# TensorE's order written out by hand around LayerNorm's transposes, in w_o's second pass and each layer's first FFN group

## The chip, the cores and the metric

The program runs on one core of one Trainium2 chip. Its time is the device time of one execution in microseconds (us), as the median of several runs. The engines are named as the profile names them: PE is TensorE (matmul and transpose), PEld its weight loads, DVE VectorE, ACT ScalarE, POOL GpSimd and SP the engine that issues most loads.

## What is computed

Two layers of a backbone over 1024 latent tokens of width 1024 (the first mixes by differential attention over 1024 + 256 tokens, the second by a centred pooling mixer), each followed by a SwiGLU FFN of width 2816. The parts that the change touches are the attention's output projection, LayerNorm behind it, and the FFN:

```python
def layer_norm(x, g, b):
    mu = jnp.mean(xf, axis=-1, keepdims=True)
    var = jnp.mean(jnp.square(xf - mu), axis=-1, keepdims=True)
    return ((xf - mu) * lax.rsqrt(var + LN_EPS) * g + b).astype(x.dtype)

x = layer_norm(ALPHA * x + g1 * y_lat, ln_g[i, 0], ln_b[i, 0])
x = layer_norm(ALPHA * x + g2 * swiglu(modulate(x, sh2, sc2), ffn_w_in[i], ffn_w_out[i]),
               ln_g[i, 1], ln_b[i, 1])
```

Everything is float32.

## The kernel before, in words

**Data.** The residual stream is `zT`, transposed: eight tiles of 128 features (index k or d), 1024 tokens along. Tokens are worked in two chunks of 512. A product takes float32 operands as two float32r parts, a rounded one and the rest (`parts`, L385: ACT casts the high part on L386, DVE subtracts for the low part on L387), and is three matmuls for each 128x128 block of weights (`mm3`, L669: high by high L670, high by low L671, low by high L672). `form` makes both parts of a weight half into one of three buffers `aop`; the raw weights come by SP's loads into six buffers `raw`.

**w_o.** The attention's projection runs in two passes of eight tiles d, the first over tokens 0 to 511, the second over 512 to 1023. One tile is 24 matmuls on two weight halves q; DVE adds it to `zT` (`accumulate`, L714).

**LayerNorm.** `ln_rows` takes one block of 128 tokens: eight PE transposes of `zT` into two banks `ln` (L558), statistics on DVE (L559, L562), a power on POOL (L564), `nb` on DVE (L566), and ACT writes the normalised rows `xn` (L568). `features` turns four such blocks back for one feature tile k (four transposes, L587, one bank), and ACT reads this bank twice: modulated for the FFN (L596) and as the new `zT` (L591). There are four `ln` banks, which rows and features share, and four `mm` banks for products.

**The FFN.** `ffn` runs eleven groups g of two column tiles. Each half s of a group is a two-by-two scheme of seven products p0 to p6 instead of eight, on seven forms of the modulated input, `H[0]` to `H[6]`. A product with one form is 12 matmuls. p0 and p1 need only H[0] and H[1], which come from tokens 0 to 511 (`forms_first`, L600); H[4], H[5], H[6] and later H[2] and H[3] (`forms_last`) need the rows of tokens 512 to 1023 (`forms_second`, L611). In group 0 the program therefore has p0 and p1 of both halves and then p0 and p1 of group 1's halves (`early`), and behind these `forms_second`; p4, p5, p6, p2 and p3 follow, then the output products on `quad` tiles. `Made` loads the first weights during w_o's second pass (layer 0) or the pooling mixer (layer 1) and casts their halves into `made`; in layer 0 for groups 0 and 1, in layer 1 for group 0 alone, so that there the early products take `aop` buffers.

**What sets the order.** Each engine runs its instructions in the order in which the built program holds them. A scheduler makes this order when the program is closed: it takes what its own model has as ready, by priority of the program text. An instruction of which `keep_in_program_order` is asked stands behind the instruction that the program text put before it on the same engine; this sets an order and adds no wait.

In layer 0 the text has rows 0 to 3 (`rows_of(0, 4)`) ahead of w_o's second pass, and behind each tile d of it `forms_first` for k = d and one step of `Made`.

## Time and profile before

| | |
|---|---|
| time, median of 3 runs | 2355.43 us (2353.51 to 2359.13) |
| the profiled execution's own time | 2353.65 us |
| its span | 2351.8 us |
| mean granted clock of PE | 0.984 |
| PE busy | 2253.2 us (96%), 11552 matmuls and transposes |
| DVE, ACT, POOL busy | 70%, 39%, 24% |
| the chain that ended last | PE 28%, DVE 3%, ACT 1% |

The span is the stretch of the execution that the profile covers. A row of the timeline has the start in us from the span's beginning, the duration, the engine, the line and the operation with output and input; a bracket gives the time for which the engine stood idle before it, and the instruction that ended this. A matmul's row lasts until its result is out, so that rows that follow each other overlap; the distance between two starts is what one costs. A windows row gives the busy time of each engine in one stretch; PEclk is the clock granted to PE as a share of 2.4 GHz.

### The profile page before, as it was taken

The numbers are of one execution on the slowest core, as the hardware profiler recorded it, in microseconds if no ns is written. First come the engines' busy times: TensorE is split into PE (matmuls) and PEld (weight loads), VectorE is DVE, ScalarE is ACT, GpSimd is POOL, SyncE is SP. The second block draws the span as 40 slices with busy tenths as digits, with TensorE's granted clock in tenths as the row PEclk, the third lists the DMA queues.
The fourth block names the chain that finished last, engine by engine and source line by source line (L and its number), as shares of the span: only waits on it lengthen the run. The fifth ranks groups of instructions, "written<-read, shape, count | busy, mean of one in ns | idle before, by whom it ended". The sixth has DMA issues, their size and how long they took to land. (4 is left out here: it accounts for less than half of the span.)

```text
span 2351.8 us, 30315 instructions
## 1 busy us (share of the span) xinstructions
PE 2253.2 (96%) x11552; PEld 1908.6 (81%) x11552; DVE 1641.9 (70%) x2478; ACT 927.6 (39%) x1599; POOL 567.4 (24%) x570
## 2 busy tenths in 40 slices
PE   5989999999999997999999999999799999999997
PEld 5878887999998785888887888897588888888886
DVE  6653626998996538877777777765776666666678
ACT  3213115787885346222222222436622222222242
POOL 3531312444443212111102111113031111111112
PEclk9999999999999998999999999999899999999999
DMA  7866746423221421322323222211021111111112
GB/s 287 271 197 218 237 134 185 111 82 88 77 63 69 156 72 44 99 82 90 90 90 117 90 90 89 70 35 53 18 72 54 54 54 54 52 49 52 50 50 90
DMA packets 98817, 231.50 MB, mean 98 GB/s; under 512 B 9200, under 2 KB 25712, under 8 KB 97648
## 3 DMA queue, kind: packets, MB, share of 16 engines
q1 hardware_dynamic: 76592, 205.45, 27.6%
q10 hardware_dynamic: 22080, 24.12, 3.7%
q8 instruction: 91, 1.49, 0.3%
q14 instruction: 54, 0.44, 0.1%
HBM read 201.22 MB, written 28.31 MB: 98 GB/s over the span
## 5 line engine op out<-in xcount | busy, mean ns | idle before, releaser
L386 ACT CAST aop<-raw 128x512 fp32r<-128x512 f32 x364 | 225.9, 622 | 682.2 <-PE mm L672 611.5
L670 PE MATMUL mm<-H,aop 128*128 128x512 f32 x1184 | 463.2, 391 | 11.5 <-ACT H L386 10.7
L672 PE MATMUL mm<-H,aop 128*128 128x512 f32 x1184 | 462.1, 391 | 1.2 <-DVE aop L387 1.2
L671 PE MATMUL mm<-H,aop 128*128 128x512 f32 x1184 | 462.4, 391 | 0.0
L387 DVE TENSOR_TENSOR aop<-raw,aop 128x512 fp32r<-128x512 f32 x364 | 272.2, 750 | 118.1 <-ACT aop L386 116.8
L714 DVE SCALAR_TENSOR_TENSOR zT<-mm,g,zT 128x512 f32<-128x512 f32 (+1 forms) x384 | 271.4, 722 | 69.8 <-PE mm L672 67.2
L670 PEld LDWEIGHTS mm<-H,aop 128*128 128x128 f32 x1184 | 223.3, 189 | 59.9 <-ACT H L386 12.2
L672 PEld LDWEIGHTS mm<-H,aop 128*128 128x128 f32 x1184 | 223.1, 188 | 49.7 <-DVE aop L387 3.5
L671 PEld LDWEIGHTS mm<-H,aop 128*128 128x128 f32 x1184 | 223.3, 189 | 47.2 <-DVE H L387 0.9
L670 PE MATMUL mm<-quad,aop 128*128 128x512 f32 x608 | 237.9, 391 | 1.2 <-DVE zT L714 1.1
L671 PE MATMUL mm<-quad,aop 128*128 128x512 f32 x608 | 237.1, 390 | 1.9 <-DVE quad L387 1.9
L672 PE MATMUL mm<-quad,aop 128*128 128x512 f32 x608 | 235.9, 390 | 0.0
L427 DVE TENSOR_REDUCE mx<-s 128x1 f32<-128x1280 f32 x128 | 190.5, 1490 | 49.9 <-PE s L424 44.9
L424 PE MATMUL s<-kk,qd 128*128 128x512 f32 (+1 forms) x768 | 183.2, 374 | 3.5 <-ACT e L430 2.9
L430 ACT ACTIVATE e<-s,mx 128x1280 f32<-128x1280 f32 x128 | 170.1, 1329 | 22.6 <-DVE mx L427 22.5
L793 POOL TENSOR_TENSOR s<-raw 128x512 f32<-128x512 f32 x40 | 52.8, 1319 | 486.5 <-DMA raw<-in_w_in 428.8
L424 PEld LDWEIGHTS s<-kk,qd 128*128 128x128 f32 x768 | 136.3, 191 | 28.0 <-ACT e L430 4.0
L455 PE MATMUL misc<-vv,at 128*128 128x128 f32 x1280 | 153.5, 275 | 0.5 <-ACT at L449 0.5
L455 PEld LDWEIGHTS misc<-vv,at 128*128 128x128 f32 x1280 | 148.0, 192 | 0.8 <-ACT at L449 0.8
L433 POOL TENSOR_SCALAR e<-e,sm 128x1280 f32<-128x1280 f32 x64 | 88.0, 1375 | 244.9 <-DVE sm L431 232.2
L671 PEld LDWEIGHTS mm<-quad,aop 128*128 128x128 f32 x608 | 114.2, 188 | 26.5 <-DVE quad L387 3.5
L670 PEld LDWEIGHTS mm<-quad,aop 128*128 128x128 f32 x608 | 114.2, 188 | 26.1 <-issue 1.5
(188 smaller groups left out, 4005.7 us busy)
## 6 DMA issues: line engine op xcount, KB each, us to landing
gw<-in_w_mod SPq DMA_DIRECT2D x96, 512.0 KB, 4.5
raw<-in_w_in SPq DMA_DIRECT2D x90, 512.0 KB, 3.8
raw<-in_w_out SPq DMA_DIRECT2D x48, 512.0 KB, 3.5
qd<-q_d SPq DMA_DIRECT2D x64, 256.0 KB, 5.8
kk<-k_d SPq DMA_DIRECT2D x8, 1280.0 KB, 6.3
wr<-in_w_qk SPq DMA_DIRECT2D x18, 512.0 KB, 5.7
k_d<-ot ACTq DMA_DIRECT2D x32, 256.0 KB, 4.4
q_d<-ot ACTq DMA_DIRECT2D x32, 256.0 KB, 4.9
```

The costliest lines, as they stand in the source:

```text
L386: S.copy(hi, src)
L387: (eng or V).tensor_tensor(lo, src, hi.bitcast(F32), ALU.subtract)
L424: PE.matmul(ps[:, lo_:hi_], lhsT=self.qd[:, m, s, q0:q0 + P], rhs=self.kk[:, m, lo_:hi_], start=(s == 0), stop=(s == 1))
L427: V.tensor_reduce(mx, ps[:, 0:TA], axis=AX.X, op=ALU.max, negate=True)
L430: S.activation(e, ps[:, 0:TA], AF.Exp, bias=mx, accum_out=sm)
L433: G.tensor_scalar(e, e, sm, 1.0, ALU.mult, ALU.mult)
L455: PE.matmul(av, lhsT=self.at[:, kb, :], rhs=self.vv[:, kb, :], start=(kb == 0), stop=(kb == NTT - 1))
L670: PE.matmul(p_, lhsT=wh, rhs=xh, start=first, stop=False)
L671: PE.matmul(p_, lhsT=wh, rhs=xl, start=False, stop=False)
L672: PE.matmul(p_, lhsT=wl, rhs=xh, start=False, stop=last)
L714: V.scalar_tensor_tensor(zT[:, d, cs], p_, gate[:, d:d + 1], zT[:, d, cs], ALU.mult, ALU.add)
L793: G.tensor_tensor(S1, r1[:, 0:4], r1[:, 4:8], ALU.add)
```

## The change

Four things in the text, all on PE's order; no arithmetic is changed, added or removed.

- `pin` asks for the text's order on the transposes and on `mm3`'s matmuls while `pinned` is set.
- In w_o's second pass, rows 0 and 1 follow tile d=0, rows 2 and 3 tile d=1, and the features follow from tile d=2 on (two feature tiles each at d=2 and d=3, then one each).
- In group 0 of each layer's FFN, rows 4 and 5 stand behind the first p0, rows 6 and 7 behind both[0]'s p1, the features of i=0 and 1 behind both early p0, those of i=2 and 3 behind both[1]'s p1.
- `forms_456` is split off `forms_second` and stands ahead of the last early p1.

```diff
@@ -533,6 +533,12 @@
         return psL.tile([P, 512], F32, name="ln", tag="ln")
 
     zT = pz.tile([P, KT, T], F32, name="zT", tag="zT")
+    pinned = [False]
+
+    def pin(ins):
+
+        return tc.keep_in_program_order(ins) if pinned[0] else ins
+
     chunk = [slice(0, 512), slice(512, 1024)]
 
     def ct():
@@ -555,7 +561,7 @@
         for hf in range(2):
             p_ = lbank()
             for j in range(4):
-                PE.transpose(p_[:, j * P:(j + 1) * P], zT[:, hf * 4 + j, t0:t0 + P], ident)
+                pin(PE.transpose(p_[:, j * P:(j + 1) * P], zT[:, hf * 4 + j, t0:t0 + P], ident))
             V.bn_stats(st[:, hf, :], p_)
             pp.append(p_)
         mv = pf.tile([P, 2], F32, name="mv", tag="mv", bufs=4)
@@ -584,7 +590,7 @@
     def features(rows, k):
         p_ = lbank()
         for t, r in enumerate(rows):
-            PE.transpose(p_[:, t * P:(t + 1) * P], r[:, k * P:(k + 1) * P], ident)
+            pin(PE.transpose(p_[:, t * P:(t + 1) * P], r[:, k * P:(k + 1) * P], ident))
         return p_[:, 0:len(rows) * P]
 
     def to_x(k, cs, li, p_):
@@ -608,13 +614,12 @@
             to_x(k, chunk[0], li, p_)
             put(H, k % 4, k // 4, H[2][:, k, :], G)
 
-    def forms_second(li, M, H):
-
-
-        rows = rows_of(4, 8)
-        H[3] = phh.tile([P, KT, 512], F32, name="hB", tag="H3")
-        H[5:7] = [h_form(s) for s in range(5, 7)]
-        for i in range(4):
+    def forms_second(li, M, H, rows, idx):
+
+
+        if H[3] is None:
+            H[3] = phh.tile([P, KT, 512], F32, name="hB", tag="H3")
+        for i in idx:
             for k in (i, i + 4):
                 p_ = features(rows, k)
                 modulated(H[3][:, k, :], k, p_, M)
@@ -622,7 +627,9 @@
             t2, h12, h22 = H[2][:, i, :], H[3][:, i, :], H[3][:, i + 4, :]
             V.tensor_tensor(t2, h12, t2, ALU.subtract)
             V.tensor_tensor(t2, h22, t2, ALU.subtract)
-        H[4] = h_form(4)
+
+    def forms_456(H):
+        H[4:7] = [h_form(s) for s in range(4, 7)]
         for i in range(4):
             put(H, i, 4, H[2][:, i, :])
         for i in range(4):
@@ -667,9 +674,9 @@
         return gt
 
     def mm3(p_, wh, wl, xh, xl, first, last):
-        PE.matmul(p_, lhsT=wh, rhs=xh, start=first, stop=False)
-        PE.matmul(p_, lhsT=wh, rhs=xl, start=False, stop=False)
-        PE.matmul(p_, lhsT=wl, rhs=xh, start=False, stop=last)
+        pin(PE.matmul(p_, lhsT=wh, rhs=xh, start=first, stop=False))
+        pin(PE.matmul(p_, lhsT=wh, rhs=xl, start=False, stop=False))
+        pin(PE.matmul(p_, lhsT=wl, rhs=xh, start=False, stop=last))
 
     class Made:
 
@@ -738,12 +745,17 @@
         if d in (1, 4):
             gemv(1, d // 4)
     g2 = gate_vector(0, 5, "g2_0")
-    rows = rows_of(0, 4)
     made = Made(0, True)
+    rows = []
     for d in range(KT):
         w_o(d, 512, 512)
-        forms_first(0, M0, H, rows, [d])
+        pinned[0] = True
+        if d < 2:
+            rows += rows_of(2 * d, 2 * d + 2)
+        else:
+            forms_first(0, M0, H, rows, [range(0, 2), range(2, 4), [4], [5], [6], [7]][d - 2])
         made.step()
+    pinned[0] = False
 
     def ffn(l, gate, li, M, H, made, beside=None, after=None):
         class Half:
@@ -868,23 +880,34 @@
             if g == 0 or last:
 
                 both = [Half(2 * g, s, sg) for s in range(2)]
-                for h in both:
-                    h.p0()
-                sg0 = ct()
-                o = [h.p1_(ct() if h.s else None, sg0) for h in both][1]
                 if last:
+                    for h in both:
+                        h.p0()
+                    sg0 = ct()
+                    o = [h.p1_(ct() if h.s else None, sg0) for h in both][1]
                     keep = phh.tile([P, 2, 2, 512], F32R, name="keep", tag="H0")
                     for j in range(2):
                         S.copy(keep[:, j], at[1][j])
                 else:
 
+                    pinned[0] = True
                     early = [Half(2, s, None) for s in range(2)]
-                    for h in early:
-                        h.p0()
+                    early_forms = bool(early[0].forms)
+                    both[0].p0()
+                    rows = rows_of(4, 6)
+                    both[1].p0()
+                    sg0 = ct()
+                    both[0].p1_(None, sg0)
+                    rows += rows_of(6, 8)
+                    early[0].p0()
+                    early[1].p0()
+                    forms_second(li, M, H, rows, range(0, 2))
+                    o = both[1].p1_(ct(), sg0)
+                    forms_second(li, M, H, rows, range(2, 4))
                     early_sg = ct()
-                    early_o = [h.p1_(ct() if h.s else None, early_sg) for h in early][1]
-                    forms_second(li, M, H)
-                    early_forms = bool(made.forms.get((1, 0, 0)))
+                    early[0].p1_(None, early_sg)
+                    forms_456(H)
+                    early_o = early[1].p1_(ct(), early_sg)
                 if last:
                     for h in both:
                         h.sums()
@@ -900,6 +923,7 @@
                 for h in both:
                     h.p2()
                 at += [h.p3() for h in both][1]
+                pinned[0] = False
             else:
                 sg += [quad(F32), quad(F32)]
                 for s in range(2):
```

PE in w_o's second pass, at its beginning. L558 (L564 in the changed text) are the transposes of rows, L587 (L593) those of features; onH is the attention's output. Before:

```order
L672 MATMUL mm<-onH_2693,aop 128x512
L558 MATMUL ln<-ident,zT 128x128 x16
L670 MATMUL mm<-onH_2695,aop 128x512
...
L558 MATMUL ln<-ident,zT 128x128 x4
L670 MATMUL mm<-onH_2695,aop 128x512
L558 MATMUL ln<-ident,zT 128x128 x8
L671 MATMUL mm<-onH_2696,aop 128x512
```

In the changed program:

```order
L679 MATMUL mm<-onH_2695,aop 128x512
L564 MATMUL ln<-ident,zT 128x128 x16
L677 MATMUL mm<-onH_2695,aop 128x512
...
L564 MATMUL ln<-ident,zT 128x128 x16
L677 MATMUL mm<-onH_2695,aop 128x512
...
L593 MATMUL ln<-ident,xn 128x128 x8
```

The first 16 transposes stood directly behind the first pass and the second 16 within tile d=0; now one whole tile of 24 matmuls stands ahead of each 16, and another ahead of the first features.

PE in group 0 of layer 0's FFN. H is a form, made a weight half. Before, behind eight products:

```order
L672 MATMUL mm<-H_7570,made 128x512
L558 MATMUL ln<-ident,zT 128x128 x32
L587 MATMUL ln<-ident,xn 128x128 x32
L670 MATMUL mm<-H_8197,aop 128x512
L671 MATMUL mm<-H_8197,aop 128x512
```

In the changed program, with products between (12, then 24, then 24, then 12 matmuls, of which each "..." leaves out the rest):

```order
L677 MATMUL mm<-H_7653,made 128x512
...
L564 MATMUL ln<-ident,zT 128x128 x16
L677 MATMUL mm<-H_7653,made 128x512
...
L564 MATMUL ln<-ident,zT 128x128 x16
...
L593 MATMUL ln<-ident,xn 128x128 x16
L677 MATMUL mm<-H_7654,made 128x512
...
L593 MATMUL ln<-ident,xn 128x128 x16
```

The 64 transposes stood in one piece behind all eight products; now they are four blocks of 16 with products between them, and two products stand behind the last block.

ACT in group 0 of layer 1's FFN. L783 (L795) copies p0's result, L827 (L839) is the Silu, hB the modulated rows, the numbered H are H[4] (14248), H[5] (14249) and H[6] (14250), aop a weight half. Before:

```order
L783 COPY ct<-mm 128x512
L386 CAST aop<-raw 128x512 x2
L827 ACTIVATE ct<-ct 128x512
L386 CAST aop<-raw 128x512
L568 ACTIVATE xn<-ln,nb,mv 128x512 x8
L596 ACTIVATE hB<-ln,bm_13312,gm_13310 128x512
L591 ACTIVATE zT<-ln,lnb,lng 128x512
```

In the changed program:

```order
L602 ACTIVATE hB<-ln,bm_13312,gm_13310 128x512
L597 ACTIVATE zT<-ln,lnb,lng 128x512
L839 ACTIVATE ct<-ct 128x512
L386 CAST H_14248<-h 128x512 x4
L386 CAST H_14249<-hB 128x512 x4
L386 CAST H_14250<-h 128x512 x3
L386 CAST aop<-raw 128x512 x2
L386 CAST quad<-ct 128x512
```

The halves of p4's weights (aop), cast ahead of the eight xn before, now stand behind the hB and zT evictions and behind eleven casts of H.

## Rows read from the trace of the kernel before

**Rows 1.** The page, part 1: busy time, share and instructions.

```profile
PE 2253.2 (96%) x11552; PEld 1908.6 (81%) x11552; DVE 1641.9 (70%) x2478; ACT 927.6 (39%) x1599; POOL 567.4 (24%) x570
```

**Rows 2.** Windows, layer 0 (busy us of each engine, PEclk, DMA share, GB/s).

```profile
800.00:810.00 10.00, 5.28 (x19) 4.36 (x18) 5.17 (x13) 1.00 (x3) 4.93 (x5) 0.66 0.11 40
820.00:830.00 10.00, 10.00 (x49) 8.25 (x48) 5.17 (x7) 6.33 (x12) 2.71 (x2) 1.00 0.38 108
...
880.00:890.00 10.00, 5.71 (x34) 4.99 (x32) 6.85 (x17) 2.79 (x4) 1.11 (x2) 0.75 0.00 0
...
900.00:910.00 10.00, 4.79 (x16) 3.38 (x14) 9.63 (x17) 10.00 (x19) 0.00 (x0) 0.66 0.00 1
```

**Rows 3.** Windows, layer 1.

```profile
1670.00:1680.00 10.00, 5.87 (x23) 3.79 (x21) 8.18 (x13) 10.00 (x17) 0.00 (x0) 0.50 0.01 2
1680.00:1690.00 10.00, 8.70 (x25) 6.63 (x26) 9.13 (x16) 8.21 (x17) 0.00 (x0) 0.64 0.00 0
```

**Rows 4.** Timeline of PE, layer 0 (start, us, line, operation, idle before).

```profile
799.29 1.03 PE L558 MATMUL ln<-ident,zT 128*128 128x128 f32 x8
805.04 1.97 PE L558 MATMUL ln<-ident,zT 128*128 128x128 f32 x8 [4.72 <-DVE zT L714]
...
858.23 0.48 PE L670 MATMUL mm<-H,made 128*128 128x512 f32 x1
...
880.13 1.91 PE L558 MATMUL ln<-ident,zT 128*128 128x128 f32 x16
886.03 3.68 PE L558 MATMUL ln<-ident,zT 128*128 128x128 f32 x16 [3.99 <-ACT xn L568]
892.31 4.01 PE L587 MATMUL ln<-ident,xn 128*128 128x128 f32 x20 [2.60 <-ACT xn L568]
...
905.55 0.79 PE L670 MATMUL mm<-H,aop 128*128 128x512 f32 x1 [5.21 <-ACT H L386]
...
908.97 0.40 PE L671 MATMUL mm<-H,aop 128*128 128x512 f32 x1
...
937.34 0.39 PE L670 MATMUL mm<-quad,aop 128*128 128x512 f32 x1
...
943.65 0.50 PE L671 MATMUL mm<-quad,aop 128*128 128x512 f32 x1 [0.48 <-DVE quad L387]
```

**Rows 5.** Timeline of PE, layer 1.

```profile
1634.81 0.48 PE L670 MATMUL mm<-H,made 128*128 128x512 f32 x1
...
1681.30 0.79 PE L670 MATMUL mm<-H,aop 128*128 128x512 f32 x1 [4.75 <-ACT H L386]
...
1686.91 0.51 PE L670 MATMUL mm<-H,aop 128*128 128x512 f32 x1
...
1721.57 0.50 PE L671 MATMUL mm<-quad,aop 128*128 128x512 f32 x1 [1.46 <-DVE quad L387]
```

**Rows 6.** Timeline of DVE, layer 0.

```profile
803.63 0.69 DVE L803 TENSOR_TENSOR raw<-raw 128x512 f32<-128x512 f32 x1 [5.52 <-POOL raw L711]
804.24 0.75 DVE L714 SCALAR_TENSOR_TENSOR zT<-mm,g,zT 128x512 f32<-128x512 f32 x1
...
894.97 0.69 DVE L623 TENSOR_TENSOR h<-hB,h 128x512 f32<-128x512 f32 x1 [2.64 <-ACT hB L596]
...
905.56 2.49 DVE L387 TENSOR_TENSOR H<-h,H 128x512 fp32r<-128x512 f32 x4
```

**Rows 7.** Timeline of ACT, layer 0.

```profile
829.78 0.62 ACT L386 CAST made<-raw 128x512 fp32r<-128x512 f32 x1 [1.61 <-DMA raw<-in_w_in]
...
885.20 2.79 ACT L568 ACTIVATE xn<-ln,nb,mv 128x512 f32<-128x512 f32 x4 [6.16 <-DVE mv L563]
...
894.16 0.78 ACT L596 ACTIVATE hB<-ln,bm,gm 128x512 f32<-128x512 f32 x1
...
904.78 2.27 ACT L386 CAST H<-h 128x512 fp32r<-128x512 f32 x4
```

**Rows 8.** Timeline of SP's issues, layer 0.

```profile
825.35 0.33 SPq L693 DMA_DIRECT2D raw<-in_w_in  x1
```

## Prediction

> **What bounds the kernel now.** I read the page's busy shares first: TensorE (PE) is busy 96% of the span [rows 1], so only the places where PE waits, or runs at a low clock, can give anything. The table of 10 us windows shows where they are in layer 0: one around 800, where PE is busy 5.28 of 10 us, and one from 880 to 910, with 5.71 to 4.79, both with granted clocks of 0.66 to 0.75; at 820, in between, PE is full at clock 1.00 [rows 2]. Layer 1 has one such place; its worst windows are those from 1670 to 1690 [rows 3]. They are the places where LayerNorm turns rows on PE, and the PE timeline names each wait: 4.72 us for DVE's zT at 805, then 3.99 for xn, 2.60 for xn and 5.21 for H between 880 and 906 [rows 4]; in layer 1, 4.75 for H at 1681 [rows 5]. The rows of DVE and ACT say what stands behind these waits [rows 6, 7].
>
> **Unit prices.** A product is 12 matmuls. From the first FFN matmul at 858.23 to the first transpose at 880.13 PE runs 8 products [rows 4], so 21.90 / 96 = 0.228 us a matmul and 2.74 us a product. A block of 16 transposes takes 1.91 us and one of 8 takes 1.03 [rows 4]: 0.88 for 8 more, 0.11 each. Where the clock is down the same block of 8 takes 1.97 [rows 4]. A DVE pass over 128x512 starts every 0.60 us and an ACT cast every 0.52 (four in 2.49 and in 2.27, the last one with an overhang of 0.1 to 0.2) [rows 6, 7]. The 16 evictions of the second forms (hB and zT in turn) run from 894.16 to 904.78, 0.66 each [rows 7].
>
> **The change, stage by stage.** No instruction is added or removed. SP's and POOL's orders are the same in both programs; PE's order changes, and with it DVE's and ACT's, which the scheduler still makes. For each stage I take the time that PE needs if it never waits, the loss before, and the loss that I expect to stay.
>
> *A, w_o's second pass* (799.29 to 858.23, 58.9 us [rows 4]). PE's work is 192 matmuls at 0.228 and 64 transposes at 0.11, 50.8 us; lost now: 8.1. The 4.72 us wait is for the last first-pass zT, which DVE writes at 804.24 because it stands behind L803, which sat 5.52 us for POOL's sums [rows 6]. POOL's order doesn't change, so zT still comes at 805.0. Now the product d=0 (5.5 us) stands ahead of these transposes and ends at 804.8; the transposes that read the last zT rows come 0.4 later, so this wait is covered. What is late next is the row chain, from transposes over statistics to the last xn: from 880.13 to 887.99 it took 7.9 us [rows 4, 7], with two passes of DVE for the FFN in it (1.2 us), so 6.7 without. The cover is 1.75 + 5.47 = 7.2 us at each of the two steps (banks for rows 2 and 3; then the features of d=2). But in the new order ACT's casts of "made" stand ahead of xn, and these wait for a load. In the old trace such a load was issued at 825.35 and its cast started at 829.78 [rows 7, 8], 4.4 us; the buffer for it comes free when DVE ends d=1's second weight half, which I put at 806.1 (zT, two halves). So ACT casts at 810.5 (two, 1.1 us), and xn of row 0 ends at 813.0: rows 2 and 3 wait for banks some 1.6 us. The next such load goes out at 814.6, is cast at 819.0, and with two casts for "made", one weight half and four xn behind it the last xn ends at 823.8, where PE arrives at 820.8: 3 us. Waits of 4.6 stay. After a wait of 3.99 us transposes ran at half rate (3.68 for 16), after one of 1.46 the first matmul took 0.50 us, not the 0.79 that it took after 5.21 [rows 4, 5]; 3 is nearer the first, so I add the price of a restart. It is 1.8 us in the one place (7 starts from 905.55 to 908.97 take 3.42 instead of 1.60) and 2.9 in the other (12 from 1681.30 to 1686.91 take 5.61 instead of 2.74) [rows 4, 5]; 2.3 here. Loss that stays: 6.9. **Gain 1.2**; bounds: -2 (another 3 us late at the loads) and 8 (all covered).
>
> *B, layer 0's first group* (858.23 to 943.65, 85.4 us, where PE last waits for quad [rows 4]). PE's work: 18 products 49.3, 64 transposes 7.0, and the output products from 937.34 to that wait of 0.48, 5.8 [rows 4]: 62.1. Lost now: 23.3. Times below are from the first p0. Rows 4 and 5 are turned at 2.7, and xn is done by 9.5; both[0].p1_ ends at 10.05, so the next 16 transposes don't wait. Rows 6 and 7 have xn at 16.7; PE arrives at 17.4. After these features ACT makes 16 evictions (10.6 us) from 18.1; the second block of features meets freed banks with 0.5 us of waiting, and ACT ends at 28.8. PE is at p4 at 29.3; H4 needs a cast and a DVE pass for its low part: p4 loses 1.0. Then DVE is late: before p5[1]'s weight half its order has H4, H5 and H6 low parts (12), two L634, L829, L830, two L800, quad and L806, and the half itself, 21 passes of 0.60 from 29.7, so 42.4; PE wants it at 39.0, 3.4 us. Later waits as now, 1.0. With half a restart (DVE paces there, so a slow PE is partly hidden), 1.0, the loss that stays is 6.9. **Gain 16.4**; bounds 12 (full restarts after both waits, 3.6 us, and DVE one pass later) and 21 (only p4's wait and the later ones stay).
>
> *C, layer 1's first group* (1634.81 to 1721.57, 86.8 us [rows 5]). The same 62.1 of work; lost now: 24.7. One thing differs: Made holds only group 0's halves here, so the early products and then p4 need weight halves cast in the stretch itself. In the old order ACT cast p4's halves ahead of xn; in the new one they stand behind the evictions and behind 11 casts of H4, H5 and H6. ACT's evictions end at 29.2 after p0; a Silu and 11 casts at 0.52 and the half itself make 36.0. On DVE the low part stands behind 11 H passes, L634 and L829: 14 passes from 30.8, 39.2. PE is at p4 at 29.8, runs two matmuls when the high part comes and waits for the low one: 9.0 lost. Then a restart, 2.3, the wait for quad that is there now, 1.5 [rows 5], and 0.5 of small ones: 13.3 stays. **Gain 11.4**; bounds 4 (the late halves push p5 and p6 as well) and 17 (the high part alone decides).
>
> The rule that speaks against this sum: the Trainium skill (TensorE: Matmul & The Clock Gate, section "HAM oscillation — how this bites in real kernels") says that where waits come again and again between short bursts, every burst starts at half rate. By it the 1.6 us of A, p4's and the whole of p5's wait in B would each cost a restart too: 5.9 us more by the price above, 2332. Here 1.46 us of waiting left the rate high, and 3.99 didn't [rows 4, 5]; nothing in this trace lies between.
>
> **Sum.** 1.2 + 16.4 + 11.4 = 29.0 us, against the profiled execution's own 2353.65 us (span 2351.8): 2324.7. The median of the three runs, 2355.43, is 1.8 above that execution, so I forecast a median of 2326. Everything outside the three stages keeps its order and its lengths. About 0.2%, 4.7 us, is what a measurement can tell from no change here.
>
> **Rivals.**
> 1. *The forms are the bound, not PE's order.* The chain of evictions, casts and low parts (ACT 10.6 us, then DVE passes) is unchanged in length; if it starts no earlier than I think in layer 1, or if the late p4 halves hold p5 and p6 too, C gives 4 or nothing, A gives nothing and B 12: 12 to 16 us, 2339 to 2343. For it: DVE's passes for the forms follow each other without a gap, in 0.60 steps [rows 6]. Against: they start at 894.97 only because ACT's first eviction came at 894.16 [rows 6, 7], 35.9 us after p0, and it now comes at 18.1. 18%.
> 2. *All is covered.* Then 8 + 21 + 17 = 46 us, 2309, when both lists of passes are shorter than I count. Against it: every pass in the two lists of B and C stands in DVE's order. 7%.
> 3. *Slower: the clock falls.* In the pinned stretches PE turns rows in short blocks between products and has several waits; if w_o's second pass ran at 1.2 GHz throughout, its 192 matmuls would cost about 0.2 and its transposes 0.11 more each, 45 us, against a gain of 28 elsewhere: 17 slower, 2372. It decides from some 29 us of extra time, two thirds of that pass. For it: 8 transposes at 1.97 after the first wait [rows 4]. Against: at 820 to 830, with four transposes between products, the granted clock was 1.00, the 2.4 GHz level, and PE was busy 10 of 10 us [rows 2]. 3%. (The rule of the Trainium skill's page TensorE: Matmul & The Clock Gate, above, is the mechanism of this rival at its mildest.)
> 4. *The change doesn't do what it says:* the scheduler's old order already hid this, or DVE and ACT, whose order isn't pinned, give all of it back. PE's listing does show the blocks apart. Within 4.7 us of 2355: 2%.
>
> **How the numbers follow.** My forecast holds 70%, with its own range of 2314 to 2338; the rivals have 18, 7, 3 and 2. The bounds of the stages sum to gains of 14 and 46 us. All three won't be at the same end, so 16 to 44: 2311 to 2339, which leaves out most of rival 1's upper half, rival 3 and the end of rival 2, some 2 in 10. Faster by over 0.2%: 70 + 18 + 7 = 95%; the same 2%; slower 3%.
>
> **What would show it.** In the changed kernel PE should wait nowhere for zT at the start of w_o's second pass, and up to 3 us for xn ahead of d=2's features. In layer 0's group PE should have no wait for xn at all, some 1 us at p4 for H, and some 3 us at p5[1] for the weight half of L387. In layer 1 the longest wait should be p4's, for weight halves and not for H, about 9 us, and the windows there should show a clock under 1. I am wrong if w_o's pass takes more than 59 us, if p4 in layer 0 still starts 40 us or more after p0 (it starts 47.3 after it now [rows 4]), or if the clock is below 1 in several windows of w_o's pass.

## The result, and the profile after

The changed kernel takes 2325.45 us, median of four runs (2323.77 to 2327.2); the kernel before, beside it, 2356.22. The ratio is 0.9872, 95% interval 0.9859 to 0.9884: 30.8 us less, where 29 and a median of 2326 were forecast. The profiled execution took 2323.77 us (span 2322.0, 29.8 less than before).

The profile page's part 1, of the changed kernel:

```profile
PE 2240.8 (97%) x11552; PEld 1903.8 (82%) x11552; DVE 1635.9 (70%) x2478; ACT 925.8 (40%) x1599; POOL 566.9 (24%) x570
```

Every engine has the instructions of before [rows 1], and DVE, ACT and POOL nearly the busy time; PE's is 12.4 us less for the same 11552, in line with less time at the low clock (mean granted clock 0.99, before 0.984). The new code shifts the line numbers by 6 to 12: transposes of rows are L564 now (L558 before), those of features L593 (L587), the three matmuls of a block L677 to L679 (L670 to L672), xn L574, `zT` of w_o L721; L386 and L387 are as they were. The timeline of PE in layer 0, from w_o's second pass to the first group's last wait:

```profile
804.90 1.91 PE L564 MATMUL ln<-ident,zT 128*128 128x128 f32 x16
...
814.12 1.32 PE L564 MATMUL ln<-ident,zT 128*128 128x128 f32 x8 [0.53 <-ACT xn L574]
...
821.80 0.55 PE L593 MATMUL ln<-ident,xn 128*128 128x128 f32 x3 [0.90 <-ACT xn L574]
823.66 1.33 PE L593 MATMUL ln<-ident,xn 128*128 128x128 f32 x5 [1.31 <-ACT xn L574]
...
855.69 0.48 PE L677 MATMUL mm<-H,made 128*128 128x512 f32 x1
...
879.38 0.66 PE L593 MATMUL ln<-ident,xn 128*128 128x128 f32 x4 [0.46 <-ACT zT L597]
...
886.39 0.50 PE L678 MATMUL mm<-H,aop 128*128 128x512 f32 x1 [0.63 <-DVE H L387]
...
898.42 0.79 PE L679 MATMUL mm<-H,aop 128*128 128x512 f32 x1 [3.33 <-DVE aop L387]
...
925.25 0.50 PE L678 MATMUL mm<-quad,aop 128*128 128x512 f32 x1 [0.67 <-DVE quad L387]
```

Where [rows 4] have 4.72 us for zT, 3.99 and 2.60 for xn and 5.21 for H, there is now one wait over 1.5 us, 3.33, and it is for another thing: the low part of p5's weight half. w_o's second pass begins at 799.44 (the transposes at 804.90 less d=0's 24 matmuls), so it takes 56.25 us to the first p0 at 855.69, where it took 58.94; the group takes 69.56 to 925.25, where it took 85.42. The same of layer 1:

```profile
1616.48 0.48 PE L677 MATMUL mm<-H,made 128*128 128x512 f32 x1
...
1652.76 0.79 PE L677 MATMUL mm<-H,aop 128*128 128x512 f32 x1 [5.97 <-ACT aop L386]
1656.29 0.79 PE L679 MATMUL mm<-H,aop 128*128 128x512 f32 x1 [2.31 <-DVE aop L387]
...
1691.69 0.50 PE L678 MATMUL mm<-quad,aop 128*128 128x512 f32 x1 [1.08 <-DVE quad L387]
```

75.21 us instead of 86.76 [rows 5]. What stays is p4's wait, 5.97 us for the cast of its weight half and 2.31 for the low part. The gains are 2.7, 15.9 and 11.6, 30.1 in all; the spans differ by 29.8.

The windows of 10 us with PE, PEld, DVE, ACT and POOL, the granted clock, the DMA share and GB/s, where waits are left:

```profile
820.00:830.00 10.00, 7.79 (x31) 6.10 (x31) 4.33 (x8) 9.12 (x15) 3.51 (x3) 0.83 0.34 106
...
880.00:890.00 10.00, 9.37 (x42) 7.37 (x41) 10.00 (x18) 10.00 (x18) 0.00 (x0) 1.00 0.00 1
890.00:900.00 10.00, 6.67 (x27) 5.17 (x26) 10.00 (x17) 3.71 (x7) 0.00 (x0) 0.92 0.00 0
900.00:910.00 10.00, 10.00 (x42) 8.16 (x41) 10.00 (x18) 6.45 (x12) 0.00 (x0) 0.91 0.52 159
...
1650.00:1660.00 10.00, 4.93 (x12) 3.46 (x13) 9.24 (x16) 4.88 (x10) 0.00 (x0) 0.52 0.00 0
```

From 880 to 910 DVE is busy 10 of 10 us: in layer 0's group it sets the pace now. ACT's and DVE's rows give the chain behind each wait that is left, w_o's pass first:

```profile
810.39 1.14 ACT L386 CAST made<-raw 128x512 fp32r<-128x512 f32 x2 [4.68 <-DMA raw<-in_w_in]
811.44 1.44 ACT L574 ACTIVATE xn<-ln,nb,mv 128x512 f32<-128x512 f32 x2
...
819.93 1.14 ACT L386 CAST made<-raw 128x512 fp32r<-128x512 f32 x2 [3.27 <-DMA raw<-in_w_in]
...
822.82 1.45 ACT L574 ACTIVATE xn<-ln,nb,mv 128x512 f32<-128x512 f32 x2
...
1651.96 1.27 ACT L386 CAST aop<-raw 128x512 fp32r<-128x512 f32 x2
```

```profile
804.53 0.74 DVE L721 SCALAR_TENSOR_TENSOR zT<-mm,g,zT 128x512 f32<-128x512 f32 x1
...
897.69 0.68 DVE L387 TENSOR_TENSOR aop<-raw,aop 128x512 fp32r<-128x512 f32 x1
...
1655.56 0.68 DVE L387 TENSOR_TENSOR aop<-raw,aop 128x512 fp32r<-128x512 f32 x1
```

The casts of `made` stood idle for a load, 4.68 and 3.27 us, with xn behind them. p5's low part in layer 0 is DVE's pass at 897.69; p4's halves in layer 1 are ACT's casts at 1651.96 and DVE's pass at 1655.56.

### The profile page after: what moved, and what is told of

The parts are those of the page before. It is cut to its first block, busy times and chain, and to the rows that moved or that the text cites. A ratio compares the mean times of both kernels' runs of the same rounds, so it can differ in the third digit from the quotient of the medians.

```text
span 2322.0 us, 30311 instructions
## 1 busy us (share of the span) xinstructions
PE 2240.8 (97%) x11552; PEld 1903.8 (82%) x11552; DVE 1635.9 (70%) x2478; ACT 925.8 (40%) x1599; POOL 566.9 (24%) x570
## 5 line engine op out<-in xcount | busy, mean ns | idle before, releaser
L386 ACT CAST aop<-raw 128x512 fp32r<-128x512 f32 x364 | 226.3, 623 | 683.2 <-PE mm L679 613.9
L677 PE MATMUL mm<-H,aop 128*128 128x512 f32 x1184 | 462.7, 391 | 6.0 <-ACT aop L386 6.0
L679 PE MATMUL mm<-H,aop 128*128 128x512 f32 x1184 | 462.8, 391 | 5.6 <-DVE aop L387 5.6
L387 DVE TENSOR_TENSOR aop<-raw,aop 128x512 fp32r<-128x512 f32 x364 | 268.8, 740 | 116.0 <-ACT aop L386 114.8
L721 DVE SCALAR_TENSOR_TENSOR zT<-mm,g,zT 128x512 f32<-128x512 f32 (+1 forms) x384 | 271.6, 721 | 71.5 <-PE mm L679 68.5
L677 PEld LDWEIGHTS mm<-H,aop 128*128 128x128 f32 x1184 | 223.3, 189 | 52.6 <-ACT aop L386 6.4
L679 PEld LDWEIGHTS mm<-H,aop 128*128 128x128 f32 x1184 | 223.1, 188 | 52.8 <-DVE aop L387 6.8
L677 PE MATMUL mm<-quad,aop 128*128 128x512 f32 x608 | 238.1, 392 | 1.1 <-DVE zT L721 1.1
L679 PE MATMUL mm<-quad,aop 128*128 128x512 f32 x608 | 236.1, 390 | 0.2 <-DVE aop L387 0.2
L677 PEld LDWEIGHTS mm<-quad,aop 128*128 128x128 f32 x608 | 114.2, 188 | 25.9 <-issue 1.5
```

The source lines that it names most:

```text
L386: S.copy(hi, src)
L387: (eng or V).tensor_tensor(lo, src, hi.bitcast(F32), ALU.subtract)
L677: pin(PE.matmul(p_, lhsT=wh, rhs=xh, start=first, stop=False))
L679: pin(PE.matmul(p_, lhsT=wl, rhs=xh, start=False, stop=last))
L721: V.scalar_tensor_tensor(zT[:, d, cs], p_, gate[:, d:d + 1], zT[:, d, cs], ALU.mult, ALU.add)
```

## The experiments

The text ahead of w_o's second pass is the same in all these kernels, but this stretch ends between 799.1 and 804.5 us in their traces. A median of four runs moves with it, so what an edit does is read from the three stages of its trace (us; w_o's second pass, then the first group of each layer to PE's last wait for quad). There is one trace of each kernel. The intervals of the ratios reach some 3 us to either side, and only e2's lies clear of the changed kernel's. What the other edits gain or lose beside the changed kernel is therefore shown by stages of single traces, and not by run times:

| kernel | w_o's pass | layer 0 | layer 1 | sum | median | ratio to before (95%) |
|---|---|---|---|---|---|---|
| before | 58.9 | 85.4 | 86.8 | 231.1 | 2356.2 | |
| changed | 56.3 | 69.6 | 75.2 | 201.0 | 2325.45 | 0.9872 (0.9859 to 0.9884) |
| e1 text only | 53.0 | 72.4 | 72.7 | 198.1 | 2324.2 | 0.9865 (0.985 to 0.988) |
| e2 w_o only | 54.4 | 86.1 | 86.0 | 226.5 | 2350.2 | 0.9973 (0.9964 to 0.9983) |
| e3 FFN only | 58.1 | 69.6 | 74.7 | 202.4 | 2326.8 | 0.9879 (0.9864 to 0.9894) |
| e4 late tile | 51.2 | 69.5 | 74.8 | 195.4 | 2323.55 | 0.9862 (0.9847 to 0.9876) |
| e5 H6 on POOL | 53.8 | 71.7 | 74.5 | 200.0 | 2325.0 | 0.987 (0.9856 to 0.9885) |
| e6 early halves | 53.3 | 69.6 | 73.6 | 196.5 | 2321.65 | 0.9858 (0.9841 to 0.9875) |
| e7 e4 + e5 + e6 | 51.2 | 70.8 | 74.9 | 196.8 | 2321.6 | 0.986 (0.9845 to 0.9875) |
| e8 halves in order | 53.1 | 70.6 | 73.8 | 197.5 | 2323.3 | 0.9861 (0.9843 to 0.9878) |
| e9 p5's halves first | 53.6 | 71.3 | 74.8 | 199.7 | 2322.6 | 0.9857 (0.9842 to 0.9872) |
| e10 e4 + e8 + e9 | 51.2 | 70.8 | 74.8 | 196.9 | 2321.0 | 0.9854 (0.9836 to 0.9873) |
| e11 H6 not formed | 55.8 | 68.2 | 73.8 | 197.8 | 2321.4 | 0.9849 (0.9833 to 0.9865) |
| e12 e4, pins in layer 0 | 51.1 | 69.5 | 72.4 | 193.0 | 2320.7 | 0.985 (0.9835 to 0.9864) |

### What the parts do: e1, e2, e3

**e1** keeps the new order of the text and drops the pins:

```diff
-        return tc.keep_in_program_order(ins) if pinned[0] else ins
+        return ins
```

> The new order of the program's text stays, but no instruction is pinned: the scheduler is free in both stages. It then makes the same order on PE in w_o's second pass and up to the early products of the first FFN groups; only p4 to p6 of layer 0's two halves are mixed with each other. Theory A (the text's order does the work, and the pins add next to nothing): 2321 to 2328 us, beside 2325.5 of the changed kernel; w_o's second pass within 0.5 us of its 56.4, layer 0's group at 68 to 71. If mixing the halves lets PE pass by the late weight half of p5, its 3.3 us wait goes and the time is at the lower end. Theory B (without pins the blocks of transposes slip back together and the waits for xn and H return): 2345 to 2356.

Theory A: 2324.2 us. No block of transposes slipped back; the text's order does the work. Two of its stage figures missed: the pass took 53.0 us for 56.4, and layer 0's group 72.4 for 68 to 71. What differs from the pinned groups is small and of both signs: layer 0's is 2.8 us longer, layer 1's 2.5 shorter. Mixing the halves did not skip p5's wait in layer 0, as I had thought it might; there are four of 0.64 to 1.25 us in its place, three for weight halves and one for DVE's read of a product.

**e2** has w_o's pass alone, and **e3** the FFN alone (each with the other part as in the kernel before):

```diff
-        if d < 2:
-            rows += rows_of(2 * d, 2 * d + 2)
-        else:
-            forms_first(0, M0, H, rows, [range(0, 2), range(2, 4), [4], [5], [6], [7]][d - 2])
+    rows = rows_of(0, 4)
...
+        forms_first(0, M0, H, rows, [d])
```

That is e3's edit; e2 puts the old lines of the FFN's first group back in the same way:

```diff
-                    both[0].p0()
-                    rows = rows_of(4, 6)
...
+                    for h in both:
+                        h.p0()
...
+                    rows = rows_of(4, 8)
+                    forms_second(li, M, H, rows, range(0, 4))
```

> w_o's second pass as changed, with its pins; the first FFN groups as before. Theory A (the stages are independent, each gain lies in its own stretch): only the pass gains, 2.5 us, 2353 to 2355 where the kernel before has 2356; layer 0's group keeps its 85 us and layer 1's its 87. Theory B (the new order of w_o's pass also brings the FFN's first rows earlier, and so part of the group's gain): layer 0's group falls below 83 us and the time below 2351. Theory C (the pass alone costs: its waits for banks are hidden by the later stages only): over 2357.

> The first FFN groups as changed, with their pins; w_o's second pass as before. Theory A (independent stages): 15.9 and 11.6 us from the two groups, 27.5 in all, 2328 to 2330; w_o's pass 58.5 to 59.5 us, with its waits of 4.7 for zT and 4.0 for xn. Theory B (layer 0's group leans on w_o's new order): the group takes over 72 us and the time is over 2331.

Theory A for both, by the stages: each gain lies in its own stretch. e2's groups take 86.1 and 86.0 us, as before; e3's take 69.6 and 74.7, as after, and its pass 58.1. Both times missed A's range on the fast side: e2's median is 2350.2 for 2353 to 2355 (B had it below 2351, but by a gain in layer 0's group, and there is none), e3's 2326.8 for 2328 to 2330. The two gains by medians, 5.6 and 29.0, sum to 34.6 where the whole change has 30.8; with some 3 us of uncertainty on each, that neither proves nor refutes that they add exactly. e2's w_o pass is 1.9 us shorter than the same order in the changed kernel, so it gained 4.6 and not 2.5. The timeline of PE in e2, and the window from 820:

```profile
821.73 0.55 PE L593 MATMUL ln<-ident,xn 128*128 128x128 f32 x3 [0.71 <-ACT xn L574]
823.58 0.77 PE L593 MATMUL ln<-ident,xn 128*128 128x128 f32 x5 [1.31 <-ACT xn L574]
824.11 0.48 PE L677 MATMUL mm<-onH,aop 128*128 128x512 f32 x1
```

```profile
820.00:830.00 10.00, 7.98 (x41) 6.24 (x40) 4.42 (x8) 9.10 (x16) 3.52 (x3) 1.00 0.36 106
```

The waits are those of the changed kernel within 0.2 us, 0.71 and 1.31, but five transposes take 0.77 us instead of 1.33, and the next matmul 0.48. The granted clock of that window is 1.00 here (the 2.4 GHz level) and was 0.83 there. The changed kernel's trace had drawn the worse of two outcomes. Eight traces have this order in the pass: the two in which the clock fell, of the changed kernel and of e11, are the longest at 56.3 and 55.8 us; the other six take 53.0 to 54.4.

### The wait in w_o's pass: e4

```diff
             self.todo += [(self.sums, s) for s in range(2)]
+            if early:
+                t = self.todo
+                self.todo = [t[0], t[1], (self.none,), (self.none,), t[4], t[5], t[2], t[3]]
...
```

(`none` is a step that does nothing.)

> The changed kernel, with the tile steps of Made's second tile moved from d=2 and 3 of w_o's second pass to d=6 and 7, so that ACT's casts of "made" no longer stand ahead of xn and the w_o loads go out in a row. Theory A (the waits in w_o's pass are those of xn behind casts that wait for a load): the waits of 0.5, 0.9 and 1.3 us for xn go, and with them the fall of the clock that followed in one of the two traces; w_o's pass falls from 54.4 to 56.3 down to 52 to 53, the time to 2321 to 2324 where the changed kernel has 2325.5. Theory B (xn is late by its own chain from the statistics, not by the casts): the waits stay, 2325 to 2327. A miss of another kind: the late tile is not ready when layer 0's first products need it, and a wait for "made" stands at the group's start.

Theory A. ACT's xn has no cast ahead of it now; the timeline of ACT and the windows of e4:

```profile
815.95 2.79 ACT L574 ACTIVATE xn<-ln,nb,mv 128x512 f32<-128x512 f32 x4 [5.25 <-DVE nb L572]
...
821.88 3.01 ACT L574 ACTIVATE xn<-ln,nb,mv 128x512 f32<-128x512 f32 x4 [2.11 <-DVE nb L572]
```

```profile
810.00:820.00 10.00, 9.99 (x61) 8.39 (x60) 8.54 (x21) 4.43 (x7) 1.48 (x2) 1.00 0.16 52
820.00:830.00 10.00, 10.00 (x50) 8.36 (x49) 4.20 (x11) 8.00 (x13) 3.06 (x4) 1.00 0.36 107
```

xn waits for its own statistics (`nb`), and PE doesn't wait at all in these windows (busy 9.99 and 10.00 of 10 us). The pass takes 51.2 us; 50.8 is what the prediction worked out for PE without any wait. Three later kernels with this edit repeat it (51.1 to 51.2). The late tile was ready in time: layer 0's group is unchanged, 69.5. The edit also lets w_o's loads go out in a row, so what it shows is that the late tile's load and casts, taken together, were the cause.

### p5's wait in layer 0: e5, e9, e11

**e5** gives H6's low parts to POOL (`G` is POOL, as `S` is ACT):

```diff
-            put(H, i, 6, h21)
+            put(H, i, 6, h21, G)
```

> The changed kernel, with the low parts of H6 formed by POOL and not by DVE: four DVE passes of 0.60 us fewer ahead of p5's weight half in each layer; POOL takes 1.3 us for such a pass. Theory A (p5's wait is DVE's list of passes): in layer 0 its wait falls from 3.3 us to 0.9 and the clock holds, the group takes 66 to 67 us where it took 69.6; in layer 1 three of the four passes stand ahead of p4's low part, but its high part comes at its own time, so 1.8 us at most, 73.4. Time 2320 to 2323. Theory B (POOL and DVE slow each other, or H6 comes late by POOL's 1.3 us passes and p6 waits): the group keeps 69 to 71, 2325 or more.

Theory B: the group takes 71.7 us, 2.1 longer. PE, DVE and POOL of e5, in this order:

```profile
896.02 0.69 PE L679 MATMUL mm<-H,aop 128*128 128x512 f32 x1 [1.92 <-DVE aop L387]
905.11 0.50 PE L679 MATMUL mm<-H,aop 128*128 128x512 f32 x1 [1.77 <-DVE aop L387]
```

```profile
893.10 1.18 DVE L387 TENSOR_TENSOR quad<-ct,quad 128x512 fp32r<-128x512 f32 x1
...
894.81 1.15 DVE L387 TENSOR_TENSOR aop<-raw,aop 128x512 fp32r<-128x512 f32 x1
895.89 3.56 DVE L649 TENSOR_TENSOR quad<-hB,h 128x512 f32<-128x512 f32 x4
```

```profile
888.96 8.13 POOL L387 TENSOR_TENSOR H<-h,H 128x512 fp32r<-128x512 f32 x4 [19.06 <-ACT H L386]
```

POOL took 8.13 us for four passes, 2.03 each in the mean; in w_o's pass, beside a DVE that is busy 4 to 5 of 10 us, such a pass took 1.28 to 1.30. DVE's passes beside it took 1.18, 1.15 and 3.56 for four, where the same ones take 0.68, 0.68 and 2.48 in the changed kernel: 2.1 us of the 2.4 that the edit took off DVE are lost again. DVE's passes that read a product (L812, L818) kept their 0.68. The Trainium skill (SBUF — State Buffer, section "Who interferes with whom") says that a DVE instruction with two inputs from SBUF contends with a GpSimd instruction that reads SBUF, and that one with at most one such input, outside the two-port modes, doesn't. The trace agrees in that the slowed ones all have two and that those with one kept their time. Not every pass with two was slowed, though: the three that DVE started between 888.9 and 890.7 (H5's last, two of L641) kept 0.60 us from start to start, and there it was POOL's first pass that took 2.99. And two waits of 1.92 and 1.77, each followed by matmuls at half rate, cost more than one of 3.33.

**e9** moves p5's halves ahead of H6's forms, with no pass less:

```diff
                 for h in both:
                     h.p4()
+                if not last:
+                    for h in both:
+                        h.forms[5] = form(h.r1[:, 0:4])
+                    forms_6(H)
```

(`forms_6` is the last loop of `forms_456`, split off.)

> The changed kernel, with p5's weight halves formed ahead of H6's forms in both layers; nothing is taken off DVE, its passes only change places. Theory A (p5 waits because of the order of DVE's list, and the slack is in what stands ahead of it: H6, the sums and quad): p5's wait of 3.3 us in layer 0 falls under 1 and the clock holds there; p6 may wait 1 to 2 us for H6 or its halves. Layer 0's group falls from 69.6 to between 65 and 67; layer 1's, where p4's wait hides the same, stays at 73.5 to 75.5; time 2320 to 2323. Theory B (DVE is full, so a pass that moves ahead only shows its wait at the next product): waits at p6 of 3 us and over, the group over 68.5, time over 2324.

Theory B by the stages; the median, 2322.6, lies in A's range and not over 2324. p5's wait is gone, and p6's halves are late instead; PE and DVE of e9 (two lines are added above, so L679 is L681, and L649 is L651):

```profile
901.84 0.80 PE L681 MATMUL mm<-H,aop 128*128 128x512 f32 x1 [4.26 <-DVE aop L387]
```

```profile
898.70 2.49 DVE L651 TENSOR_TENSOR quad<-hB,h 128x512 f32<-128x512 f32 x4
901.10 1.29 DVE L387 TENSOR_TENSOR aop<-raw,aop 128x512 fp32r<-128x512 f32 x2
```

DVE has no gap from 885 to 905. The whole wait moved one product on; but four passes for the last forms (L651), which PE wants only after p6, stand right ahead of p6's halves. Whether it helps to put these behind was not tried, so "DVE is full" is shown for its order, not for every order.

**e11** leaves out the four subtractions, so that DVE is rid of them without POOL; ACT gets four more casts for them:

```diff
-            put(H, i, 6, h21)
+            S.copy(H[6][:, i, :], h21)
+            S.copy(H[6][:, 4 + i, :], h21)
```

> The changed kernel without the subtractions that form H6's low parts: ACT writes a second cast of the same rows in their place (0.52 us each), so the low parts of H6 hold the wrong numbers; DVE has four passes fewer in each layer and POOL none more. It tells what ate the gain of giving these passes to POOL. Theory A (DVE's sum of passes bounds layer 0's group, and POOL's passes slowed DVE's): p5's wait falls from 3.3 us to 0.5 to 1.5, nothing of that comes back at p6, the group falls from 69.6 to between 65.5 and 67.5. Theory B (something else holds p5 and p6, the halves' three buffers or ACT): waits of 3 us or more in sum at p5 and p6, the group 69 to 71. Layer 1: p4's cast stands behind two or three more casts, its low part behind fewer passes: 74 to 77. Time 2319 to 2323 by A, 2325 by B.

Between the two theories. Layer 0's group takes 68.2 us, 1.4 less than in the changed kernel, and layer 1's 73.8, just under the 74 to 77 expected; the waits of PE and the windows of e11:

```profile
898.77 0.50 PE L680 MATMUL mm<-H,aop 128*128 128x512 f32 x1 [0.69 <-DVE aop L387]
906.29 0.50 PE L680 MATMUL mm<-H,aop 128*128 128x512 f32 x1 [1.46 <-DVE aop L387]
```

```profile
890.00:900.00 10.00, 9.31 (x40) 7.11 (x39) 10.00 (x18) 8.33 (x17) 0.00 (x0) 1.00 0.00 0
900.00:910.00 10.00, 8.54 (x35) 6.09 (x34) 9.79 (x17) 6.66 (x12) 0.00 (x0) 1.00 0.34 107
```

p5's wait fell by 2.64 us, a little more than four passes (2.4), but 1.46 came back at p6. The clock held at 1.00 through both. e5 took the same passes off DVE, and its group is 3.5 us longer: that is POOL's company and the restarts behind e5's longer waits; how it divides between them was not measured.

### p4's wait in layer 1: e6, e8, e12

**e6** and **e8** form layer 1's weight halves earlier, e8 in PE's order (early[0] first). This is e8's edit:

```diff
+                    if not early_forms:
+                        early[0].forms[1] = form(early[0].r0[:, 4:8])
                     forms_second(li, M, H, rows, range(0, 2))
...
+                        early[1].forms[1] = form(early[1].r0[:, 4:8])
                     forms_second(li, M, H, rows, range(2, 4))
...
+                        for h in both:
+                            h.forms[4] = form(h.r0[:, 0:4])
                     forms_456(H)
```

> The changed kernel, with layer 1's weight halves of the last early product and of p4 formed ahead of the second half of the forms (layer 0 has them from Made). Theory A (p4's wait of 6.0 and 2.3 us in layer 1 is the cast and the low part standing behind H's): that wait falls under 2 us. DVE has the same passes to do ahead of p5, so some of it comes back there, as in layer 0: layer 1's group falls from 75.2 to between 69 and 71, the time to 2319 to 2322. Theory B (the bound is the length of ACT's and DVE's lists, not their order): the wait moves whole to p5 or to H4, the group stays at 74 to 76, 2325.

> The changed kernel, with layer 1's weight halves formed in the order in which PE wants them: early[0]'s and early[1]'s second half ahead of the features, both halves of p4 ahead of H4 to H6. (The earlier run formed early[1]'s and p4's ahead of early[0]'s, and with three buffers for halves early[0]'s then came last.) Theory A (only the order was wrong there): no wait at early[0]'s product; p4 waits some 2 us for H4 behind the two low parts, p5 some 3 us as in layer 0; group 70.5 to 72.5 instead of 75.2, time 2321 to 2324. Theory B (the buffers decide: p4's second half has none until PE has used one, and waits behind H again): a wait of over 3 us at p4's second product, group 73 to 75.

Neither theory held as it was put: layer 1's group takes 73.6 and 73.8 us, 1.6 and 1.4 less (e8's lies in the range of B, but without B's wait; both medians lie in A's ranges). PE of e6, then of e8:

```profile
1645.82 0.79 PE L677 MATMUL mm<-H,aop 128*128 128x512 f32 x1 [5.20 <-ACT aop L386]
```

```profile
1646.97 0.50 PE L677 MATMUL mm<-H,aop 128*128 128x512 f32 x1 [1.28 <-ACT H L386]
...
1659.39 0.79 PE L679 MATMUL mm<-H,aop 128*128 128x512 f32 x1 [4.85 <-DVE aop L387]
```

In e6 the half of early[0]'s product came last of three and cost 5.20 us. e8 has the order right and p4 waits 1.28 and 1.09 us, but then p5 waits 4.85, with DVE's passes ahead of its half. The wait of p4 has become one of p5.

**e12** takes e4's edit and keeps the pins in layer 0 alone:

```diff
                     early_forms = bool(early[0].forms)
+                    pinned[0] = early_forms
```

> Late tile of Made, and the pins kept in w_o's pass and in layer 0's group alone; layer 1's group is the scheduler's, in the new order of the text. Each part has been seen to take: w_o's pass 51.2, layer 0's group 69.5, layer 1's 72.7. If they add: 193.4 for the three where the changed kernel has 201.0, time 2318 to 2321. If layer 1's 72.7 was an accident of one execution: 74 to 75.5 there, 2320 to 2323.

The parts add: 193.0 us where 193.4 were expected, and a median of 2320.7 us (2319.27 to 2321.76), the lowest, though not clear of e10's 2321.0. Layer 1's 72.4 repeats e1's 72.7, so that was no accident of one execution. What layer 1 gains is seen on PE of e12:

```profile
1652.33 0.80 PE L677 MATMUL mm<-H,aop 128*128 128x512 f32 x1 [6.17 <-ACT aop L386]
1652.92 0.63 PE L678 MATMUL mm<-H,aop 128*128 128x512 f32 x1
1653.35 0.63 PE L677 MATMUL mm<-H,aop 128*128 128x512 f32 x1
...
1655.69 0.60 PE L679 MATMUL mm<-H,aop 128*128 128x512 f32 x1 [0.43 <-DVE aop L387]
```

Pinned, PE ran two matmuls of p4 and stood 2.31 us for the low part. Free, it runs six that need only the high parts of the weights and stands 0.43; they also use up the time at half rate.

### All together: e7, e10

e7 is e4, e5 and e6 in one; e10 is e4, e8 and e9.

> The three edits together: late tile of Made, low parts of H6 on POOL, early halves of p4 in layer 1. If each of them is right and they are independent: w_o's pass 52 to 53, layer 0's group 66 to 67, layer 1's group 67 to 69, time 2312 to 2316. If the waits only move from one of DVE's lists to the next: not under 2320.

> Late tile of Made, layer 1's halves in PE's order, p5's halves ahead of H6, together. With theory A of each: w_o's pass 51 to 52, layer 0's group 65 to 67, layer 1's group 67 to 70; beside the changed kernel's 56.3, 69.6 and 75.2 that is 12 to 18 us, time 2308 to 2314. If DVE's sum of passes is the bound in the groups, only w_o's part and 2 to 3 us of layer 1 come: 2317 to 2321.

Both came out near their second case: w_o's part adds fully (51.2), the groups give nothing (70.8 and 74.9, 70.8 and 74.8), not even the 2 to 3 us of layer 1 that e10's second case had. In e10 layer 1's p4 waits 1.27 and 1.10, p5 0.93 and p6 3.34 us: the list of DVE's passes shows its length at one product or another.

## Why the prediction was right

Time, stages and mechanisms hold: 2325.45 for 2326, a sum of gains of 30.1 for 29.0, and e2 and e3 show each gain in its own stretch. That the two come within 1.1 us of each other is partly luck: it rests on a trace in which w_o's pass was the longest of eight with this order. With the 53.0 to 54.4 us of six others, A would have gained 4.6 to 6.0 us for the predicted 1.2.

**A, w_o's pass, was mis-sized.** Predicted gain 1.2, measured 2.7. The zT wait is covered as said (zT at 804.53, PE at 804.90, no wait). The casts of `made` came at 810.39 (810.5) and 819.93 (819.0) and the last xn ended near 824.3 (823.8), and PE was there at 820.9 (820.8). The loss that stays was put at 6.9 and is 5.45 (56.25 less the 50.8 of work). Of its terms, the banks for rows 2 and 3 cost about 1.3 us for 1.6: PE is through with d=1's matmuls at 812.12 and starts the next at 815.20, 3.08 us for 16 transposes that take 1.75. The row of PE shows 0.53 of it in one wait; the weight loads show all four waits, these two and two of 0.25 between and behind them:

```profile
812.27 0.42 PEld L564 LDWEIGHTS ln<-ident,zT 128*128 128x128 f32 x4 [0.42 <-ACT xn L574]
...
814.12 0.42 PEld L564 LDWEIGHTS ln<-ident,zT 128*128 128x128 f32 x4 [0.77 <-ACT xn L574]
```

The features cost 0.90 and 1.31 instead of 3. The restart was put at 2.3; it cost about 1.7 in the changed kernel's trace and nothing in e2's (1.9 us between the two passes, 0.2 of it waits). e4 shows the cause of these losses by removing it: without the casts ahead of xn, the pass is 51.2, so the prediction's upper bound of 8 for this stage was there to be had.

**B, layer 0's group**, 69.56 us for the predicted 69.0. PE has no wait for xn; p4 waits 0.63 for H (1.0), p5 3.33 for its weight half (3.4), quad 0.67 (1.0). The list of 21 passes was right too: they run from 885.65 to the half's at 897.69. Only the half restart was too cheap: eight matmuls from 898.42 to 901.93 cost 1.7 us more than at the full rate, not 1.0. That p5's wait is DVE's list of passes is shown by e11, which takes four off it; e9 says that moving the half forward within the list only hands the wait on.

**C, layer 1's group**, 75.21 for 75.4. p4's wait is 5.97 and 2.31, 8.3 in all with two matmuls between (9.0), for weight halves and not for H, and the window shows a clock of 0.52, as was to be seen.

**The rivals.** The forms (rival 1) bound what is left, but not the change: they start earlier, as the point against this rival had it. Layer 0's second evictions begin with this row of ACT, 18.1 us after p0, where it was 35.9 [rows 7]:

```profile
873.82 0.82 ACT L602 ACTIVATE hB<-ln,bm,gm 128x512 f32<-128x512 f32 x1
```

DVE's 30 us without a gap come after that, from 880 to 910. Not all was covered (rival 2); the clock never fell for a whole pass (rival 3): the one window below 1 in w_o's pass is 820 to 830, at 0.83.

**The rule of the Trainium skill** (TensorE: Matmul & The Clock Gate, section "HAM oscillation — how this bites in real kernels"), as the prediction applied it to every wait, would have given 2332. The trace agrees for p5's wait: after 3.33 us the matmuls ran at half rate, as they did after 1.92 in e5. After 0.46, 0.53, 0.63 and 0.67 us the rate stayed high, after 0.71 with 1.31 in e2 too, and after 1.46 in e11, so not each wait costs a restart. The rows do hold a wait between the prediction's 1.46 and 3.99, of 2.60 [rows 4]; its transposes ran at half rate, but so did those ahead of it, and it decides nothing.

## What to carry to other kernels

Where a nearly full engine waits for a row chain, put independent products into the text ahead of the transposes that need it; the cover needed is the chain's own length, read from its rows, plus what stands ahead of it on the other engines. Then list, on the engine that feeds the waiting one, every pass ahead of the operand that is wanted next: the wait that stays can be priced from this list, and moving a single pass forward only hands the wait on once that engine has no gaps. Look for loads ahead of the chain too: a cast that waited for one held xn back behind it, and with it out of the way this pass took 51.1 to 51.2 us in four traces, where it took 53.0 to 56.3 in eight.

## What the runs showed of the hardware that was not expected

**The clock after short waits is not fixed by the waits.** In one order of instructions, 0.90 and 1.31 us, three transposes apart, brought PE to half rate (1.33 us for five transposes); 0.71 and 1.31 in e2 did not (0.77). In e11 waits of 0.63 and 1.31, no longer than e2's, brought it down (1.04 for five). A single wait of 1.30 (e5) or 1.12 (e6) in the same place left it high, and so did 1.28 and 1.09 one matmul apart, at p4 of e8's layer 1 (0.23 us from start to start behind them). What decides in between stays open.

**POOL beside DVE slows both.** Passes of 128x512 on POOL took 2.03 us each in the mean beside a DVE without gaps (e5) and 1.28 to 1.30 in w_o's pass; DVE's of the same time up to 1.7 times their usual length (1.18 for 0.68), though its first ones beside POOL (H5's and L641's, 0.60 apart) did not slow, and POOL's own first took 2.99. Which of the two is held when was not tried.
